# Delta rule: key and query products as half-array matmuls on the tiles where they lie, in place of keys copied into half-zero tiles

## The chip, the cores and the metric

One Trainium2 chip, one of its cores. A core has TensorE (PE in the rows, and PEld for its weight loads), VectorE (DVE), ScalarE (ACT), GpSimd (POOL) and SyncE (SP, which issues the transfers). The metric is the time of one execution on the device, in microseconds (us).

## The reference

Two blocks of two layers each, 512 positions wide. The change lies in the second block's mixer, in its third branch, the gated delta rule: 4 heads with keys, queries and values of 64 channels.

```
qc, kc, vc, bc, gc = (to_chunks(t) for t in (q, k, v, beta, g))
G = jnp.cumsum(gc, axis=-1)
L = jnp.exp(jnp.where(incl, G[..., :, None] - G[..., None, :], -jnp.inf))
kb = kc * bc[..., None]
A = jnp.where(strict, jnp.einsum('bnhtd,bnhsd->bnhts', kb, kc) * L, 0.0)
T = lax.linalg.triangular_solve(eye + A, eye, left_side=True, lower=True, unit_diagonal=True)
...
qk = jnp.where(incl, jnp.einsum('bnhtd,bnhsd->bnhts', qc, kc) * L, 0.0)
```

The two einsums, keys with keys and queries with keys, sum over the 64 channels of a head. They are what the change computes in another way. The kernel uses chunks of 128 positions, so there are 4 blocks (`b` from 0 to 3) of 4 heads (`h`).

## The kernel before

Each layer of the second block runs `second_mixer`: wide products with the weights, the second branch (`hgrn`), and then the third branch (`gdn`) woven with the first (`swa`, sliding window attention): `weave` takes one step of each generator in turn. Inside `gdn` the function `block(b)` runs for the four blocks, woven as well. The order of instructions on each engine is then set once, when the program is built, by a scheduler that works from its own estimates; on the chip each engine takes its list in that order.

Keys and queries lie with channels on the partitions: `k[0]` holds head 0 on partitions 0 to 63 and head 1 on 64 to 127, `k[1]` holds heads 2 and 3, and `q` likewise. The tiles in the rows are named `cout`. To keep the other head out of a sum over 128 partitions, the kernel copies each head's keys into a tile of its own, whose other 64 partitions are zero: `kz`, named `gk` in the rows, zeroed by GpSimd at L1400 and filled by ScalarE at L1401.

`block(b)` then does, step by step: transposes of the cumulated gates (L1438), the decay `e` (L1441 on VectorE, L1442 on ScalarE; `ge` in the rows), keys with keys (L1450), `am` from them (L1452; `gm` in the rows), transposes of `am` (L1457) with two selecting copies (L1458, L1459), queries with keys (L1463), their product with the decay (L1464), transposes of that (L1468, copied out by ScalarE at L1469), and then six doubling steps of the triangular inverse (L1476 with a copy L1477, L1481 with L1482, L1487 with L1488), all of them full 128x128 products.

Each step takes one tile from the PSUM pool `mm`, which has four tiles of 128x512 in turn: a step's products can't start before the tile that was taken four times earlier has been read out. `swa` has a pool of its own (`mx`, four tiles). Its lines in the rows: scores L1121, mask and maximum on VectorE (L1124, L1126), small vectors L1131 to L1134, the exponentials on ScalarE (L1138), normalising (L1140, L1141, L1143), transposes L1158 with copies L1160, and products with the values L1167, which use the 64 columns of one half of the array (128*64 in the rows).

A matmul of 128x128 in float32 stands as two rows' worth of records: the 16 products of L1450 in a layer are 32 records, and so are the 16 of L1463.

`hgrn`, which runs earlier in each layer, already has products of half the array: L1273 multiplies partitions 0 to 63 into one PSUM tile and 64 to 127 into another (64*128 in the rows).

Of the kernel before, what the change touches and what calls it, by code (L numbers as in the profile page):

```python
# [13 lines left out]
ALU = mybir.AluOpType  # L14
# [3 lines left out]
P = 128  # L18
SEQ = 512
# [230 lines left out]
class Net:  # L250
# [1095 lines left out]
    def gdn(self, x, cg, ba, l, out):  # L1346
        nc, V, G = self.nc, self.nc.vector, self.nc.gpsimd
        T = nc.tensor
# [14 lines left out]
        ps = self.ps("mm")  # L1363
# [24 lines left out]
        for i in range(2, 4):  # L1388
            ps = early.spread2(rn[:, :, 2 * i:2 * i + 2])
# [3 lines left out]
        rq = self.small((P, NB, 4), "grq", 2)  # L1393
        V.tensor_scalar(rq, rn[:, :, 0:4], 0.125, None, op0=ALU.mult)
        q, k, vf = x[0:2], x[2:4], x[4:6]
        kz2 = [self.big((P, 2, SEQ), "gk") for _ in range(2)]
        kz = [kz2[h // 2][:, h % 2, :] for h in range(4)]
        for h, t in enumerate(kz):
            r, n = slice(64 * (h % 2), 64 * (h % 2) + 64), slice(64 - 64 * (h % 2), 128 - 64 * (h % 2))
            G.memset(t[n, :], 0.0)  # L1400
            nc.scalar.copy(t[r, :], k[h // 2][r, :])  # L1401

        eb = self.small(sh, "geb", 2)
        V.tensor_tensor(eb, beta, eg, op=ALU.mult)
# [1 line left out]
        for i in range(2):  # L1406
            hh = slice(2 * i, 2 * i + 2)
            bc = lambda y: y[:, :, hh].unsqueeze(3).to_broadcast([P, NB, 2, 64])
            r = self.big((P, NB, 2, 128), name="grhs")
            ps = early.to_f([vf[i][:, b * P:(b + 1) * P] for b in range(NB)])  # L1410
            v4 = ps.rearrange("p (a b c) -> p a b c", a=NB, b=2)
            V.tensor_tensor(r[:, :, :, 0:64], v4, bc(beta), op=ALU.mult)
            ps = early.to_f([k[i][:, b * P:(b + 1) * P] for b in range(NB)])
            k4 = ps.rearrange("p (a b c) -> p a b c", a=NB, b=2)
            V.tensor_tensor(r[:, :, :, 64:128], k4, bc(eb), op=ALU.mult)
            t = self.t((P, NB, 2, 64), name="gkd")
# [9 lines left out]
        nb = self.small(sh, "gnb", 2)  # L1426
        V.tensor_scalar(nb, beta, -1.0, None, op0=ALU.mult)
        p4 = lambda y: y.rearrange("p (a b) -> p a b", a=4)
# [5 lines left out]
        def block(b):  # L1434
            s = slice(b * P, (b + 1) * P)
            ps = self.ps()
            for h in range(4):
                T.transpose(ps[:, h * P:(h + 1) * P], gc[:, b, h:h + 1].to_broadcast([P, P]), self.ident)  # L1438
            e = self.t((P, 4, P), name="ge")
            for h in range(4):  # L1440
                V.scalar_tensor_tensor(e[:, h, :], ps[:, h * P:(h + 1) * P], gc[:, b, h:h + 1], later, op0=ALU.subtract, op1=ALU.max)  # L1441
            nc.scalar.activation(out=e, in_=e, func=AF.Exp, scale=-1.0)  # L1442
            r0 = self.wp.tile([P, 2, 4, P], F32, tag="whi", name=self.nm("gm0"))
            r1 = self.wp.tile([P, 2, 4, P], F32, tag="wlo", name=self.nm("gm1"))
            xx, xt, am, zt = r0[:, 0], r0[:, 1], r1[:, 0], r1[:, 1]
            nc.sync.dma_start(out=r0.rearrange("p a b c -> p (a b) c"), in_=self.ident.unsqueeze(1).to_broadcast([P, 8, P]))
            yield
            ps = self.ps()
            for h in range(4):
                T.matmul(ps[:, h * P:(h + 1) * P], kz[h][:, s], kz[h][:, s], start=True, stop=True)  # L1450
            for h in range(4):
                V.scalar_tensor_tensor(am[:, h, :], ps[:, h * P:(h + 1) * P], nb[:, b, h:h + 1], e[:, h, :], op0=ALU.mult, op1=ALU.mult)  # L1452
            yield

            ps = self.ps()
            for h in range(4):
                T.transpose(ps[:, h * P:(h + 1) * P], am[:, h, :], self.ident)  # L1457
            V.copy_predicated(xx, all4(off1).bitcast(I32), am)  # L1458
            V.copy_predicated(xt, all4(lvs[0]).bitcast(I32), p4(ps))  # L1459
            yield  # L1460
            ps = self.ps()
            for h in range(4):
                T.matmul(ps[:, h * P:(h + 1) * P], q[h // 2][:, s], kz[h][:, s], start=True, stop=True)  # L1463
            V.tensor_tensor(e, p4(ps), e, op=ALU.mult)  # L1464
            yield
            ps = self.ps()
            for h in range(4):
                T.transpose(ps[:, h * P:(h + 1) * P], e[:, h, :], self.ident)  # L1468
            nc.scalar.copy(e, p4(ps))  # L1469
            QT[b] = e  # L1470
            yield

            for n in range(1, 7):
                ps = self.ps()
                for h in range(4):
                    T.matmul(ps[:, h * P:(h + 1) * P], am[:, h, :], xt[:, h, :], start=True, stop=True)  # L1476
                nc.scalar.copy(zt, p4(ps))  # L1477
                yield
                ps = self.ps()
                for h in range(4):  # L1480
                    T.matmul(ps[:, h * P:(h + 1) * P], xx[:, h, :], zt[:, h, :], start=True, stop=True)  # L1481
                V.copy_predicated(xt, all4(lvs[n]).bitcast(I32), p4(ps))  # L1482
                yield
                if n < 6:
                    ps = self.ps()
                    for h in range(4):
                        T.transpose(ps[:, h * P:(h + 1) * P], xt[:, h, :], self.ident)  # L1487
                    nc.scalar.copy(xx, p4(ps))  # L1488
                yield
            ps = self.ps()  # L1490
            for h in range(4):
                T.matmul(ps[:, h * P:(h + 1) * P], xt[:, h, :], rhs[h // 2][:, b, h % 2, :], start=True, stop=True)
            t = self.t((P, 4, P), name="guw", tag="x")
            nc.scalar.copy(t, p4(ps))
            uw[b] = t
            yield
            if b:
                ps = self.ps()
                for h in range(4):
                    p = h % 2  # L1500
                    T.matmul(ps[64 * p:64 * p + 64, (h // 2) * P:(h // 2 + 1) * P], rhs[h // 2][:, b, p, 64:128], xt[:, h, :], start=True, stop=True)
                for i in range(2):
                    nc.scalar.copy(wt[i][:, s], ps[:, i * P:(i + 1) * P])
            yield

        yield from weave(*(block(b) for b in range(NB)))

        sbd = {}
        for i in range(2):
            state = None  # L1510
            for c in range(NB - 1):
                ps = self.ps("mx")
                for p in range(2):
                    r = slice(64 * p, 64 * p + 64)
# [6 lines left out]
                else:  # L1521
                    m = self.t((P, P), name="gmt", tag="x")
                    G.memset(m, 0.0)
                    for p in range(2):
                        r = slice(64 * p, 64 * p + 64)
                        V.scalar_tensor_tensor(m[r, r], self.ident[r, r], gl[r, c, 2 * i + p:2 * i + p + 1], ps[r, 64 + 64 * p:128 + 64 * p],
                                               op0=ALU.mult, op1=ALU.subtract)
# [10 lines left out]
                for p in range(2):  # L1538
                    r = slice(64 * p, 64 * p + 64)
# [3 lines left out]
        for b in range(NB):  # L1543
            s = slice(b * P, (b + 1) * P)
# [15 lines left out]
            else:  # L1560
                t = self.t((P, 4, 64), name="got", tag="x")
                V.tensor_tensor(t, o3(po[:, 256:512]), eg[:, b, :].unsqueeze(2).to_broadcast([P, 4, 64]), op=ALU.mult)
                V.tensor_tensor(hs[:, 0], t, o3(p2[:, 0:256]), op=ALU.add)
            r = self.head_rstd(hs, (1, 4), rq[:, b:b + 1, :])
# [299 lines left out]
```

## Time and profile before

| | us |
|---|---|
| median of 3 runs | 3590.18 (3586.36 to 3591.63) |
| profiled execution, its time | 3586.55 |
| profiled execution, its span | 3584.7 |
| L1450 in one layer, TensorE | 5.51 |
| L1401 in one layer, ScalarE | 2.54 |
| L1400 in one layer, GpSimd | 2.24 |

The span runs from the first to the last instruction; 1.85 us of the profiled execution's time lie around it. The stage of the change comes twice, from 2296 us (first layer of the second block) and from 3035 us (its second layer). Rows name engine, line, operation, the tile written and those read, and in brackets the idle time of the engine before it and what ended it.

### The profile page before, as it was taken

How to read it: one execution, taken by the hardware profiler on the slowest of the kernel's cores; microseconds unless marked ns; L12 is line 12 of the kernel's file. 1: busy time of each engine (PE TensorE's matmuls, PEld its weight loads, DVE VectorE, ACT ScalarE, POOL GpSimd, SP SyncE). 2: the span in 40 equal slices, each digit the busy share in tenths (PEclk: the TensorE clock that was granted, in tenths of full speed). 3: DMA queues.
4: the chain of work that ended last, by engine and by line, in shares of the span. 5: the costliest groups of instructions: out<-in, count | busy, mean ns of one | idle time of the engine just before them, and what ended most of it. 6: DMA issues, size and time to landing. Idle time of an engine off the chain costs nothing.

```text
span 3584.7 us, 44503 instructions
## 1 busy us (share of the span) xinstructions
PE 3484.3 (97%) x17694; PEld 2901.8 (81%) x17694; DVE 1989.1 (55%) x3074; ACT 1364.5 (38%) x2231; POOL 140.5 (4%) x130
## 2 busy tenths in 40 slices
PE   9999999999999999999999998899999989999999
PEld 7888777888888888777888887788888877888887
DVE  6555665554665555674556577756333475654333
ACT  4223454323333223463223364354222453543221
POOL 0000000000000000000000003100000021000000
PEclk9999999999999999999999999899999999999999
DMA  5444212444334443202444321102333222022332
GB/s 167 141 135 129 84 32 68 142 145 128 127 100 142 146 138 100 91 15 95 146 148 137 94 77 54 62 7 75 108 98 101 78 71 68 1 71 90 100 99 83
DMA packets 114272, 349.06 MB, mean 97 GB/s; under 512 B 11536, under 2 KB 27920, under 8 KB 114064
## 3 DMA queue, kind: packets, MB, share of 16 engines
q1 hardware_dynamic: 114064, 346.21, 30.8%
q8 instruction: 140, 2.29, 0.3%
q14 instruction: 68, 0.56, 0.0%
HBM read 339.87 MB, written 2.10 MB: 95 GB/s over the span
## 4 chain that ended last, share of the span: by engine, by line
PE 87%; DVE 6%; issue 3%; ACT 2%; POOL 1%; DMA 1%; SPq 0%; POOLq 0%; DVEq 0%; ACTq 0%
PE mm L406 24%; PE mm L408 24%; PE mm L407 24%; PE mm L1481 1%; PE mm L1476 1%; PE mm L476 1%; PE mm L477 1%; PE mm L475 1%; PE mx L968 1%; DVE hacc L1279 1%; DVE wlo L382 1%; PE mm L809 1%; PE mx L948 1%; ACT sc L1138 1%; PE mx L1121 1%
## 5 line engine op out<-in xcount | busy, mean ns | idle before, releaser
L381 ACT CAST whi<-wraw 128x1024 fp32r<-128x1024 f32 (+3 forms) x540 | 553.4, 1029 | 1553.6 <-PE mm L407 1271.7
L406 PE MATMUL mm<-xh,whi 128*128 128x512 f32 (+1 forms) x2784 | 1053.3, 380 | 9.7 <-ACT whi L381 6.4
L407 PE MATMUL mm<-xl,whi 128*128 128x512 f32 (+1 forms) x2784 | 1055.8, 380 | 1.6 <-DVE xl L588 1.4
L408 PE MATMUL mm<-xh,wlo 128*128 128x512 f32 (+1 forms) x2784 | 1055.8, 380 | 0.3 <-DVE wlo L382 0.3
L382 DVE TENSOR_TENSOR wlo<-wraw,whi 128x1024 fp32r<-128x1024 f32 (+3 forms) x540 | 643.7, 1194 | 274.9 <-ACT whi L381 234.3
L406 PEld LDWEIGHTS mm<-xh,whi 128*128 128x128 f32 x2784 | 522.4, 189 | 107.8 <-ACT whi L381 6.4
L407 PEld LDWEIGHTS mm<-xl,whi 128*128 128x128 f32 x2784 | 524.9, 189 | 100.3 <-DVE xl L588 2.5
L408 PEld LDWEIGHTS mm<-xh,wlo 128*128 128x128 f32 x2784 | 524.8, 189 | 100.4 <-DVE wlo L382 3.1
L408 PE MATMUL mm<-hi,wlo 128*128 128x512 f32 (+1 forms) x1390 | 532.2, 383 | 2.1 <-DVE wlo L382 2.1
L406 PE MATMUL mm<-hi,whi 128*128 128x512 f32 (+1 forms) x1390 | 532.5, 384 | 0.2
L407 PE MATMUL mm<-lo,whi 128*128 128x512 f32 (+1 forms) x1390 | 531.8, 383 | 0.0
L408 PEld LDWEIGHTS mm<-hi,wlo 128*128 128x128 f32 x1390 | 261.3, 188 | 54.2 <-DVE wlo L382 4.2
L406 PEld LDWEIGHTS mm<-hi,whi 128*128 128x128 f32 x1390 | 261.1, 188 | 51.4 <-ACT hi L399 1.1
L407 PEld LDWEIGHTS mm<-lo,whi 128*128 128x128 f32 x1390 | 261.3, 188 | 50.3
L658 DVE SCALAR_TENSOR_TENSOR h<-mm,h 128x512 f32<-128x512 f32 x112 | 77.2, 691 | 224.2 <-PE mm L408 224.1
L1589 DVE SCALAR_TENSOR_TENSOR ada<-wraw,cond,ada 128x1024 f32<-128x1024 f32 x84 | 107.9, 1284 | 95.6 <-DMA wraw<-in_ada_w_dram 95.2
L637 DVE TENSOR_TENSOR gl<-mm,rstd 128x512 f32<-128x512 f32 x88 | 60.7, 690 | 155.1 <-PE mm L408 155.1
L636 DVE TENSOR_TENSOR silu<-mm,rstd 128x512 f32<-128x512 f32 x88 | 60.7, 689 | 145.2 <-PE mm L408 145.2
L658 DVE SCALAR_TENSOR_TENSOR h<-mm,mod,h 128x512 f32<-128x512 f32 (+1 forms) x70 | 48.9, 704 | 148.7 <-PE mm L408 148.7
L399 ACT CAST hi<-gl 128x512 fp32r<-128x512 f32 x132 | 82.2, 623 | 100.6 <-DVE gl L639 99.9
L633 DVE TENSOR_TENSOR gl<-silu,mm 128x512 f32<-128x512 f32 x44 | 30.2, 687 | 135.8 <-PE mm L408 135.8
L400 DVE TENSOR_TENSOR lo<-gl,hi 128x512 fp32r<-128x512 f32 x132 | 90.5, 686 | 15.4 <-ACT hi L399 15.4
(493 smaller groups left out, 3606.2 us busy)
## 6 DMA issues: line engine op xcount, KB each, us to landing
wraw<-in_ffn_gate_dram SPq DMA_DIRECT2D x130, 512.0 KB, 3.5
wraw<-in_ffn_up_dram SPq DMA_DIRECT2D x130, 512.0 KB, 4.0
wraw<-in_ada_w_dram SPq DMA_DIRECT2D x96, 512.0 KB, 3.7
wraw<-in_ffn_down_dram SPq DMA_DIRECT2D x96, 448.0 KB, 3.3
wraw<-in_win_f_dram SPq DMA_DIRECT2D x50, 512.0 KB, 3.5
wraw<-in_ffn_down_dram SPq DMA_DIRECT2D x48, 512.0 KB, 3.5
wraw<-in_w_out_dram SPq DMA_DIRECT2D x32, 512.0 KB, 3.5
wraw<-in_win_t_dram SPq DMA_DIRECT2D x16, 512.0 KB, 3.5
```

Of the source, the lines that this page charges most:

```text
L381: self.nc.scalar.copy(hi[:, s], raw)
L382: self.nc.vector.tensor_tensor(lo[:, s], raw, hi[:, s].bitcast(F32), op=ALU.subtract)
L399: self.nc.scalar.copy(hi, src)
L400: self.nc.vector.tensor_tensor(lo, src, hi.bitcast(F32), op=ALU.subtract)
L406: T.matmul(ps, whi, xhi, start=first, stop=False)
L407: T.matmul(ps, whi, xlo, start=False, stop=False)
L408: T.matmul(ps, wlo, xhi, start=False, stop=last)
L475: T.matmul(ps, xh[:, bs], w[0][:, s], start=k == 0, stop=False)
L636: nc.vector.tensor_tensor(sg, gate_ps, rb, op=ALU.mult)
L637: nc.vector.tensor_tensor(gg, up_ps, rb, op=ALU.mult)
L658: self.nc.vector.scalar_tensor_tensor(h, ps[:, c], scale, h, op0=ALU.mult, op1=ALU.add)
L1589: V.scalar_tensor_tensor(acc, raw, cond[:, k:k + 1], acc, op0=ALU.mult, op1=ALU.add)
```

## The change

The copies `kz` with their memsets go. Keys with keys and queries with keys are taken by a helper `scores`, which multiplies 64 partitions of `k[i]` or `q[i]` with the same 64 of `k[i]`. The two halves write into two PSUM tiles, so a step that took one tile of the pool now takes two, each half filled. Head `h` then lies in tile `h % 2` at column block `h // 2`; the four VectorE operations at L1452 read from there, and L1464 becomes two operations of 128x256 on every second head in place of one of 128x512. Behind the helper the lines are numbered by 4 and less more; the helper's matmul is L1403.

```
-        kz2 = [self.big((P, 2, SEQ), "gk") for _ in range(2)]
-        kz = [kz2[h // 2][:, h % 2, :] for h in range(4)]
-        for h, t in enumerate(kz):
-            r, n = slice(64 * (h % 2), 64 * (h % 2) + 64), slice(64 - 64 * (h % 2), 128 - 64 * (h % 2))
-            G.memset(t[n, :], 0.0)
-            nc.scalar.copy(t[r, :], k[h // 2][r, :])
+        half = slice(0, 64), slice(64, 128)
+        def scores(x, y, s):
+            pss = [self.ps() for _ in range(2)]
+            for i in range(2):
+                for r, ps in zip(half, pss):
+                    T.matmul(ps[:, i * P:(i + 1) * P], x[i][r, s], y[i][r, s], start=True, stop=True)
+            return [ps[:, 0:2 * P].rearrange("p (a b) -> p a b", a=2) for ps in pss]
...
-            ps = self.ps()
+            pss = scores(k, k, s)
             for h in range(4):
-                T.matmul(ps[:, h * P:(h + 1) * P], kz[h][:, s], kz[h][:, s], start=True, stop=True)
-            for h in range(4):
-                V.scalar_tensor_tensor(am[:, h, :], ps[:, h * P:(h + 1) * P], nb[:, b, h:h + 1], e[:, h, :], op0=ALU.mult, op1=ALU.mult)
+                V.scalar_tensor_tensor(am[:, h, :], pss[h % 2][:, h // 2, :], nb[:, b, h:h + 1], e[:, h, :], op0=ALU.mult, op1=ALU.mult)
...
-            ps = self.ps()
-            for h in range(4):
-                T.matmul(ps[:, h * P:(h + 1) * P], q[h // 2][:, s], kz[h][:, s], start=True, stop=True)
-            V.tensor_tensor(e, p4(ps), e, op=ALU.mult)
+            for ps, y in zip(scores(q, k, s), (e[:, 0:4:2, :], e[:, 1:4:2, :])):
+                V.tensor_tensor(y, ps, y, op=ALU.mult)
```

The first place is on TensorE, at the queries with keys of blocks 2 and 3. Before, `mm_17610` is block 2, `mm_17622` block 3, both whole; `ge` are the transposes of L1468, `sc` and `pt` belong to `swa`:

```order
L1463 MATMUL mm_17610<-gk_17275,cout_16971 128x128 x2
L1463 MATMUL mm_17610<-gk_17276,cout_17012 128x128 x2
L1463 MATMUL mm_17622<-gk_17275,cout_16971 128x128 x2
L1463 MATMUL mm_17622<-gk_17276,cout_17012 128x128
L1121 MATMUL mx_17616<-kz_17251,u_16788 128x256
L1121 MATMUL mx_17616<-kz_17254,u_16788 128x256
L1463 MATMUL mm_17622<-gk_17276,cout_17012 128x128
L1468 MATMUL mm_17650<-base,ge_17350 128x128 x4
L1158 MATMUL mx_17657<-base,sc_17399 128x128 x2
L1158 MATMUL mx_17668<-base,sc_17419 128x128 x4
L1167 MATMUL mx_17656<-pt_17660,av_15674 64x128
L1468 MATMUL mm_17662<-base,ge_17386 128x128 x4
```

In the change the same place reads as follows; `mm_17608` and `mm_17609` are the two halves of block 2, `mm_17622` and `mm_17623` those of block 3:

```order
L1121 MATMUL mx_17616<-kz_17254,u_16788 128x256
L1403 MATMUL mm_17608<-cout_17053,cout_16971 128x128
L1403 MATMUL mm_17608<-cout_17094,cout_17012 128x128
L1158 MATMUL mx_17659<-base,sc_17389 128x128 x2
L1403 MATMUL mm_17609<-cout_17053,cout_16971 128x128
L1403 MATMUL mm_17609<-cout_17094,cout_17012 128x128
L1158 MATMUL mx_17670<-base,sc_17409 128x128 x4
L1167 MATMUL mx_17658<-pt_17662,av_15674 64x128
L1403 MATMUL mm_17622<-cout_17053,cout_16971 128x128
L1403 MATMUL mm_17622<-cout_17094,cout_17012 128x128
L1167 MATMUL mx_17658<-pt_17662,av_15674 64x128
L1158 MATMUL mx_17685<-base,sc_17429 128x128 x3
```

Block 3's second half, `mm_17623`, follows after these and stands between products of L1158. Before, two blocks stood in one run; now four half blocks stand one by one among full-array products, and the transposes of L1468 have moved behind them.

The second place is on VectorE, where `am` is made from the keys' products. Before, the rows of the first two blocks read:

```order
L1143 TENSOR_TENSOR sc_17342<-sc_17342,wr_17361 128x512
L1452 SCALAR_TENSOR_TENSOR gm_3283_17357<-mm_17442,gnb_17335,ge_17350 128x128 x4
L1124 TENSOR_TENSOR sc_17454<-mx_17451,mats_16874 128x512
L1452 SCALAR_TENSOR_TENSOR gm_3290_17393<-mm_17457,gnb_17335,ge_17386 128x128
L1126 TENSOR_REDUCE wm_17395<-sc_17454 128x2
```

And in the change:

```order
L1143 TENSOR_TENSOR sc_17332<-sc_17332,wr_17351 128x512
L1454 SCALAR_TENSOR_TENSOR gm_3281_17347<-mm_17432,gnb_17325,ge_17340 128x128
L1454 SCALAR_TENSOR_TENSOR gm_3281_17347<-mm_17433,gnb_17325,ge_17340 128x128
L1454 SCALAR_TENSOR_TENSOR gm_3281_17347<-mm_17432,gnb_17325,ge_17340 128x128
L1454 SCALAR_TENSOR_TENSOR gm_3281_17347<-mm_17433,gnb_17325,ge_17340 128x128
L1124 TENSOR_TENSOR sc_17445<-mx_17442,mats_16874 128x512
```

Here VectorE's work stays in its place, still behind the normalising products L1143; only the tiles read have become two.

## Rows read from the trace of the kernel before

**Rows 1.** The page's chain that ended last, shares of the span by engine

```profile
PE 87%; DVE 6%; issue 3%; ACT 2%; POOL 1%; DMA 1%; SPq 0%; POOLq 0%; DVEq 0%; ACTq 0%
```

**Rows 2.** Busy time by stretches; PE, PEld, DVE, ACT, POOL, granted clock, DMA share, GB/s

```profile
2296.00:2345.00 49.00, 36.28 (x240) 30.43 (x241) 44.27 (x107) 22.58 (x59) 6.86 (x4) 0.83 0.00 1
2345.00:2400.00 55.00, 53.40 (x480) 50.11 (x476) 23.52 (x48) 35.09 (x83) 1.23 (x5) 1.00 0.01 1
```

**Rows 3.** Chain in order of time: start, length, piece; a row of the inverse

```profile
2377.71 3.57 PE mm L1476 x32
```

**Rows 4.** Timeline of ScalarE at the copies: start, length, work, idle before

```profile
2301.54 2.54 ACT L1401 COPY gk<-cout 64x512 f32<-64x512 f32 x4
2307.17 0.63 ACT L843 ACTIVATE cout<-cacc 128x512 f32<-128x512 f32 x1 [3.09 <-DVE cacc L841]
```

**Rows 5.** Timeline of GpSimd at the memsets

```profile
2184.07 2.24 POOL L1400 MEMSET gk<- 64x512 f32 x4
2186.57 1.04 POOL L1260 TENSOR_TENSOR he<-hl 128x512 f32<-128x512 f32 x1 [0.25 <-DVE hk L1265]
```

**Rows 6.** Timeline, first layer, keys with keys and VectorE around them

```profile
2317.57 5.51 PE L1450 MATMUL mm<-gk 128*128 128x128 f32 x32 [1.95 <-ACT sc L1138]
2320.96 0.17 DVE L1140 TENSOR_TENSOR wr<-wr,we 128x8 f32<-128x8 f32 x1 [0.69 <-ACT sc L1138]
2324.10 1.12 DVE L1452 SCALAR_TENSOR_TENSOR gm<-mm,gnb,ge 128x128 f32<-128x128 f32 x4
2333.38 0.17 DVE L1140 TENSOR_TENSOR wr<-wr,we 128x8 f32<-128x8 f32 x1 [0.41 <-ACT sc L1138]
```

**Rows 7.** Timeline of TensorE, first layer, queries with keys and after

```profile
2337.67 0.94 PE L1463 MATMUL mm<-gk,cout 128*128 128x128 f32 x6 [2.28 <-DVE gm L1459]
2338.44 1.03 PE L1121 MATMUL mx<-kz,u 128*128 128x256 f32 x4
2339.31 0.38 PE L1463 MATMUL mm<-gk,cout 128*128 128x128 f32 x2
2341.08 0.43 PE L1167 MATMUL mx<-pt,av 128*64 128x128 f32 x2 [0.26 <-ACT pt L1160]
2346.65 2.84 PE L1476 MATMUL mm<-gm,gm 128*128 128x128 f32 x24
```

**Rows 8.** Timeline of TensorE in `hgrn`, one half-array run between full ones

```profile
2167.10 0.34 PE L475 MATMUL mm<-whi,xh 128*128 128x392 f32 x1
2167.37 1.16 PE L1273 MATMUL mx<-hq,hk 64*128 64x128 f32 x16
2168.47 0.44 PE L476 MATMUL mm<-wlo,xh 128*128 128x392 f32 x1
2168.75 0.34 PE L477 MATMUL mm<-whi,xl 128*128 128x392 f32 x1
2168.93 0.34 PE L475 MATMUL mm<-whi,xh 128*128 128x392 f32 x1
```

**Rows 9.** Timeline of weight loads where 128 and 64 columns change

```profile
2325.32 0.42 PEld L1158 LDWEIGHTS mx<-base,sc 128*128 128x128 f32 x4 [0.17 <-issue]
2325.90 0.41 PEld L1167 LDWEIGHTS mx<-pt,av 128*64 128x64 f32 x4 [0.17 <-issue]
```

**Rows 10.** Timeline of VectorE, one operation of 256 and one of 512

```profile
2338.09 0.43 DVE L1124 TENSOR_TENSOR sc<-mx,mats 128x256 f32<-128x256 f32 x1
2338.42 0.69 DVE L1464 TENSOR_TENSOR ge<-mm,ge 128x512 f32<-128x512 f32 x1
```

**Rows 11.** 2 us stretches of both layers, columns as in rows 2

```profile
2336.00:2338.00 2.00, 0.33 (x3) 0.33 (x4) 2.00 (x4) 0.00 (x0) 0.00 (x0) 1.00 0.00 0
3076.00:3078.00 2.00, 2.00 (x10) 1.71 (x10) 2.00 (x6) 0.00 (x0) 0.00 (x0) 0.66 0.00 0
```

**Rows 12.** Timeline of TensorE, second layer, same place as rows 7

```profile
3075.51 0.94 PE L1463 MATMUL mm<-gk,cout 128*128 128x128 f32 x6 [2.27 <-DVE gm L1459]
3085.80 2.84 PE L1476 MATMUL mm<-gm,gm 128*128 128x128 f32 x24
```

## The prediction

> **What bounds the kernel now.** I read the chain first: 87% of it is TensorE [rows 1], so time is saved or lost where TensorE's list gets shorter or longer, unless another engine is waited for at that place. The stage of the change is partly such a place, so I read it by stretches [rows 2]. From 2296 to 2345 us TensorE is busy for 36.28 of 49 us and VectorE for 44.27: here VectorE is ahead of TensorE as the bound. From 2345 to 2400 TensorE is busy for 53.40 of 55 us, and its chain runs record on record: 32 records of the inverse take 3.57 us, 0.112 each [rows 3]. What is late on TensorE when that second part begins is late at the end.
>
> The border between the two lies at the queries with keys. TensorE waits 2.28 us for VectorE's L1459, starts at 2337.67, and from then on has next to no gap [rows 7]. So each part of the change is priced by the side of 2337.67 on which it falls. The second layer has the same list and the same border, at 3075.51 [rows 12].
>
> **The copies that go.** L1401 takes 2.54 us of ScalarE, but the next work of ScalarE then waits 3.09 us for VectorE [rows 4]: worth nothing. L1400 takes 2.24 us of GpSimd, and the next L1260 starts when VectorE has read its tile, after a gap of 0.25 [rows 5]: worth nothing either. If that cover failed, the two would be worth at most 2.54 + 2.24 us a layer.
>
> **Keys with keys, before the border.** L1450 takes 5.51 us [rows 6]. It looks like the natural place for a gain, but the work behind it on VectorE doesn't start when it is done: VectorE waits for ScalarE's exponentials at 2320.96, then normalises, and takes up L1452 at 2324.10, a microsecond after the products have ended. The order on VectorE has not moved there. I take nothing. Two PSUM tiles a block mean that blocks 2 and 3 can't start before blocks 0 and 1 are read out by VectorE, where before all four were issued in one run. Block 3's products then have the time in which VectorE does block 2, four operations in 1.12 us, and take up to 1.30 (eight records and a change of shape and back, priced below): 0.2 us late. VectorE has 0.41 us in hand, in which it waits for ScalarE at 2333.38 [rows 6], so I take nothing; with that slack gone it is 0.2 us a layer.
>
> **Queries with keys, at and after the border.** Here order and trace together give the loss. Before, block 3 starts at 2337.67 and six of its eight records are out before L1121 can start at 2338.44; only two records, at 2339.31, cost anything after that: 2 x 0.112 = 0.22 us [rows 7]. In the change blocks 2 and 3 both lie behind the border, since their PSUM tiles are those of blocks 0 and 1, which L1464 must read first; and they lie there as four runs of two matmuls, each between products of another shape.
>
> What such a run costs, `hgrn` shows [rows 8]. From the start of the full product at 2167.10 to that of the second full one after the half-array run, at 2168.75, 1.65 us pass. Two full products of 392 columns are in it, 0.18 each (2168.75 to 2168.93). That leaves 1.29 for 16 half-array records. One by one they would take 1.79, yet the row has all 16 within 1.16, so they run in pairs, one from each half, 8 x 0.112 = 0.89; the other 0.40 is the price of going into the half shape and back. A run of four records, all from one half, has no partner to start with: 4 x 0.112 + 0.40 = 0.85 us. Four runs: 3.4 us. Less the 0.22 that was there: +3.2 us.
>
> The Trainium skill ("TensorEngine Tiling (Array Packing)", Theoretical Speedup) gives products whose sum runs over 64 or fewer up to twice the speed. The pairs of `hgrn` agree, 16 records in 1.16 us [rows 8]. By that rule these four runs would cost half, 4 x 0.22 = 0.9 us, and the change would cost 0.7 us a layer here and not 3.2; by the order printed above each run has one half only, so I go by the row.
>
> The order also breaks up `swa`'s products of 64 columns: seven runs of L1167 before the inverse in place of four, which is four changes of shape more, beside those already in the 0.40. A change costs TensorE 0.17 us [rows 9]: 0.7 us. Part of them fall where TensorE would wait anyway, and the wait of 0.26 for ScalarE [rows 7] goes; between 0 and 0.7 I take half, 0.35, less 0.26: +0.1. L1464 becomes two operations of 256: 2 x 0.43 - 0.69 = 0.17 us a block, 0.7 a layer on VectorE [rows 10]. It lies beside TensorE's longer list and costs nothing; without that cover it is 0.7.
>
> So +3.3 us a layer, +6.6 for two, and no stretch of TensorE's later list has a gap to swallow it [rows 2, 3].
>
> **The clock.** In the first layer TensorE is busy for only 0.33 us of the two before 2338 and keeps the clock of 2.4 GHz; in the second, at the same place, part of the stretch from 3076 runs at the level of 1.2 GHz (mean 0.66) [rows 11]. What that costs is in the rows: from the border to the inverse the first layer takes 2346.65 - 2337.67 = 8.98 us, the second 3085.80 - 3075.51 = 10.29, so 1.3 us [rows 7, 12]. The change moves two blocks' products out of the stretch ahead of the border, so TensorE does less there in both layers. I expect the first layer to lose its clock as the second does: +1.3. The same could happen after 2322, where TensorE now waits between the blocks of L1403; that is another 1.3 a layer at most, and I leave it to the range.
>
> **Sum.** 6.6 + 1.3 = 7.9 us. The profiled execution's 3586.55 us lie 3.63 below the median of the runs shown; against the median the forecast is 3590.18 + 7.9 = 3598.
>
> **Rivals.** *Hidden both ways*: the four runs fall into gaps between VectorE's operations. L1464's eight operations and the L1124 and L1126 between them pace that stretch too. For it speaks that VectorE is the busier engine up to 2345; against it that TensorE has one gap of 0.26 us there and none after. Then the change costs at most the 0.2 us a layer of the first stretch: 3590 to 3591.
>
> *The other side, faster*: the stretch of L1450 is TensorE's after all. The chain that ended last does pass through its 5.51 us. If halves paired up there and in L1463 as in `hgrn`, 64 records a layer would fall from 0.112 to 0.056: 3.6 us a layer, 7.2 in all, 3583. It decides itself at VectorE's first L1452: if that starts well before 2324.1, this is the case. VectorE's wait for ScalarE at 2320.96 speaks against it, and so does the order, which sets two matmuls of one half behind each other. The Trainium skill's rule of the twofold speed, named above, would give this case if TensorE were the bound.
>
> *Deeper loss*: the clock stays at 1.2 GHz from the waits between the blocks of keys with keys through to the inverse. Then to the 7.9 come 1.3 a layer after 2322, and the shape changes are dearer at half clock, up to 0.40 for each of the eight runs: 7.9 + 2.6 + 3.2 = 13.7, 3604.
>
> **How the numbers follow.** No change means within 0.2%, 7.2 us of 3590.18, about what a measurement of this kernel can tell. The forecast gets 0.62; its own range is +4 to +12 us, and it falls on both sides of 7.2: 0.39 slower, 0.23 the same. Hidden 0.20, all the same. Faster 0.08: 0.05 faster, 0.03 the same, since 7.2 is on the border. Deeper 0.10, slower. That is 0.05 faster, 0.46 same, 0.49 slower. The range runs from 3589, just below the hidden case, to 3604, the deeper one, and leaves out the faster case and what is beyond the deeper one, some 0.15.
>
> **What would show it.** Right: VectorE's first `am` at its old place; four separate runs of L1403 behind the border, each some 0.85 us from the product before to the product after; the inverse's first L1476 later against the border by 3 to 5 us in the first layer; granted clock below 1 around 2336 to 2342. Wrong: runs of L1403 that add less than 0.6 each, or TensorE idle between them for VectorE; `am` earlier than before; a later wait (TensorE's for L1488) that shrinks by as much as the stage grew.

## The result and the profile after

The changed kernel takes 3615.91 us (median of four runs, 3614.14 to 3620.5) against 3590.45 for the kernel before on the same chip: ratio 1.0078, 95% interval 1.0066 to 1.0089. It is 25 us slower. The forecast was 3598 with a range from 3589 to 3604; sign and place were right, the size was not.

The profiled run of after has a span of 3612.1 us, 27.4 more than before. The place is again the border between VectorE's part and TensorE's part of the stage: the wait of 2.71 us that VectorE's L1461 ends. TensorE in the first layer, at the border, at the inverse's first product and at L1492, the first product behind the inverse; then the same three in the second layer (answers to [rows 7, 12]):

```profile
2339.45 0.71 PE L1403 MATMUL mm<-cout,cout 64*128 64x128 f32 x4 [0.58 <-DVE gm L1461]
2342.87 1.22 PE L1403 MATMUL mm<-cout,cout 64*128 64x128 f32 x4 [2.71 <-DVE gm L1461]
2344.02 2.07 PE L1121 MATMUL mx<-kz,u 128*128 128x256 f32 x4
2346.03 1.22 PE L1403 MATMUL mm<-cout,cout 64*128 64x128 f32 x4
2347.18 0.69 PE L1158 MATMUL mx<-base,sc 128*128 128x128 f32 x2
2347.79 1.22 PE L1403 MATMUL mm<-cout,cout 64*128 64x128 f32 x4
...
2360.60 0.94 PE L1476 MATMUL mm<-gm,gm 128*128 128x128 f32 x6
2427.01 3.74 PE L1492 MATMUL mm<-grhs,gm 128*128 128x128 f32 x32
...
3093.76 1.22 PE L1403 MATMUL mm<-cout,cout 64*128 64x128 f32 x4 [2.71 <-DVE gm L1461]
3111.49 0.94 PE L1476 MATMUL mm<-gm,gm 128*128 128x128 f32 x6
3177.90 3.74 PE L1492 MATMUL mm<-grhs,gm 128*128 128x128 f32 x32
```

Before, L1492 stands here:

```profile
2411.37 3.74 PE L1492 MATMUL mm<-grhs,gm 128*128 128x128 f32 x32
3150.51 3.74 PE L1492 MATMUL mm<-grhs,gm 128*128 128x128 f32 x32
```

From the border to L1492 before takes 2411.37 - 2337.67 = 73.70 us and 3150.51 - 3075.51 = 75.00 [rows 7, 12]; after takes 84.14 in both layers: +10.44 and +9.14. L1492 is the better mark than L1476 here, since the change also moves the transposes L1468 partly behind the first L1476.

The border itself comes later. VectorE of after, where it makes `am` (L1454; before, L1452 of [rows 6]):

```profile
2326.79 1.12 DVE L1454 SCALAR_TENSOR_TENSOR gm<-mm,gnb,ge 128x128 f32<-128x128 f32 x4
...
2331.67 0.35 DVE L1454 SCALAR_TENSOR_TENSOR gm<-mm,gnb,ge 128x128 f32<-128x128 f32 x1 [1.47 <-PE mm L1403]
...
2334.47 1.12 DVE L1454 SCALAR_TENSOR_TENSOR gm<-mm,gnb,ge 128x128 f32<-128x128 f32 x4 [1.45 <-PE mm L1403]
```

The first `am` still follows L1143 without a wait, but VectorE then waits twice for L1403, of block 2 and of block 3. From the first `am` to the border: 2342.87 - 2326.79 = 16.08 us, before 2337.67 - 2324.10 = 13.57 [rows 6, 7], so +2.51. That is the two waits less the 0.41 us that VectorE had in hand [rows 6]: 1.47 + 1.45 - 0.41. The first `am` of the second layer, after and then before:

```profile
3077.62 1.12 DVE L1454 SCALAR_TENSOR_TENSOR gm<-mm,gnb,ge 128x128 f32<-128x128 f32 x4
```

```profile
3062.03 1.12 DVE L1452 SCALAR_TENSOR_TENSOR gm<-mm,gnb,ge 128x128 f32<-128x128 f32 x4
```

There it is 3093.76 - 3077.62 = 16.14 against 3075.51 - 3062.03 = 13.48, so +2.66.

The first layer's loss is 2.51 + 10.44 = 12.95, the second's 2.66 + 9.14 = 11.80: the two stages hold 24.75 of the 27.4 us. The rest lies ahead of the first layer's first `am`, 2326.79 against 2324.10; e3 and e6 below, which keep the copies, have it at 2326.45 and 2328.65, and no cause is shown for it.

What TensorE does there is in the windows of after: from 2298 us to the border, within that 10 us of keys with keys, and 15 us from the border on (columns as in [rows 2]):

```profile
2298.00:2342.87 44.87, 30.79 (x177) 24.02 (x177) 37.13 (x95) 17.01 (x48) 6.55 (x3) 0.72 0.00 1
2320.90:2331.10 10.20, 9.23 (x42) 6.73 (x44) 8.62 (x27) 6.20 (x16) 0.00 (x0) 0.50 0.00 0
2342.87:2357.87 15.00, 15.00 (x52) 10.18 (x53) 8.35 (x21) 2.13 (x4) 0.00 (x0) 0.50 0.00 0
```

Behind the border TensorE has work in all 15.00 us, and the granted clock is 0.50, 1.2 GHz, in all of them: 52 records. Another 10 us at that level lie ahead of it, while keys with keys run. Before, 17 us from the border have a clock of 1.00 in the first layer and 0.90 in the second:

```profile
2337.67:2354.67 17.00, 16.74 (x135) 14.85 (x136) 12.79 (x28) 11.34 (x30) 0.52 (x2) 1.00 0.01 1
3075.51:3092.51 17.00, 17.00 (x125) 15.04 (x126) 11.49 (x24) 10.48 (x29) 0.32 (x1) 0.90 0.00 1
```

The copies that went left waits of the same size: ScalarE's L843 now waits 5.54 us where it waited 3.09 [rows 4], and GpSimd's L1260 waits 2.57 where it waited 0.25 [rows 5]. After, ScalarE and then GpSimd:

```profile
2309.87 0.63 ACT L843 ACTIVATE cout<-cacc 128x512 f32<-128x512 f32 x1 [5.54 <-DVE cacc L841]
...
2188.98 1.04 POOL L1260 TENSOR_TENSOR he<-hl 128x512 f32<-128x512 f32 x1 [2.57 <-DVE hk L1265]
```

### The profile page after: what moved, and what is told of

Read it like the earlier page. It is cut to its first block, busy times and chain, and to the rows that moved or that the text cites. A ratio compares the mean times of both kernels' runs of the same rounds, so it can differ in the third digit from the quotient of the medians.

```text
span 3612.1 us, 44485 instructions
## 1 busy us (share of the span) xinstructions
PE 3508.6 (97%) x17694; PEld 2912.4 (81%) x17694; DVE 1990.0 (55%) x3082; ACT 1360.4 (38%) x2223; POOL 135.3 (4%) x122
## 4 chain that ended last, share of the span: by engine, by line
PE 87%; DVE 6%; issue 3%; ACT 2%; POOL 1%; DMA 1%; SPq 0%; POOLq 0%; DVEq 0%; ACTq 0%
PE mm L406 24%; PE mm L408 24%; PE mm L407 24%; PE mm L1481 1%; PE mm L1476 1%; PE mm L477 1%; PE mm L476 1%; PE mm L475 1%; PE mx L968 1%; DVE hacc L1279 1%; DVE wlo L382 1%; PE mm L809 1%; PE mx L1121 1%; PE mx L948 1%; PE mx L1158 1%
```

## Experiments

The change does three things to TensorE: a step takes two PSUM tiles (which also reorders its list), products have the half shape, and the granted clock falls. The theory is that the clock is the larger part of the loss; the rivals are tiles and order, and the price of changing the shape. "kk" is keys with keys, "qk" queries with keys. Each ratio is to the kernel before, measured beside the run.

| run | median us | ratio, 95% interval |
|---|---|---|
| e1 all full, two tiles a step | 3597.3 | 1.0025 (1.0016 to 1.0034) |
| e2 kk halves, qk as before | 3593.5 | 1.0008 (0.9999 to 1.0017) |
| e3 qk halves, kk as before | 3611.0 | 1.0061 (1.0047 to 1.0074) |
| e4 changed kernel, filler after every run | 3604.8 | 1.0043 (1.0029 to 1.0057) |
| e5 heads 0 and 2 halves, one tile | 3604.2 | 1.0044 (1.0030 to 1.0058) |
| e6 qk full, two tiles; kk as before | 3595.2 | 1.0018 (1.0009 to 1.0027) |
| e7 second half in swa's pool | 3602.9 | 1.0038 (1.0025 to 1.0050) |
| e8 before, copies twice | 3593.0 | 1.0012 (1.0004 to 1.0021) |
| e9 heads 0 and 2 over 65 partitions | 3591.8 | 1.0004 (0.9994 to 1.0013) |
| e10 halves, two blocks a pair of tiles | 3598.4 | 1.0024 (1.0015 to 1.0034) |
| e11 as e6, qk of blocks 2, 3 halves | 3606.5 | 1.0055 (1.0039 to 1.0071) |
| e12 as e6, qk of blocks 0, 1 halves | 3598.8 | 1.0029 (1.0020 to 1.0038) |
| e13 as e3, the wait filled | 3597.7 | 1.0018 (1.0008 to 1.0027) |
| e14 as e6, the wait filled | 3593.3 | 1.0011 (1.0002 to 1.0019) |
| e15 changed kernel, the wait filled | 3598.5 | 1.0025 (1.0015 to 1.0035) |
| e16 before, the wait filled | 3586.8 | 0.9988 (0.9979 to 0.9997) |

**Tiles and order without the half shape (e1).** The copies are kept and both operands are full again:

```
...
-                for r, ps in zip(half, pss):
-                    T.matmul(ps[:, i * P:(i + 1) * P], x[i][r, s], y[i][r, s], start=True, stop=True)
+                for p, ps in enumerate(pss):
+                    T.matmul(ps[:, i * P:(i + 1) * P], (x[i] if x is q else kz[2 * i + p])[:, s], kz[2 * i + p][:, s], start=True, stop=True)
```

> The copies of the keys stay, and every product is a full-array product again, but each step of scores writes two half-filled PSUM tiles: TensorE's list has the same order as in the changed kernel, row for row. Theory A (shape and clock): what costs 25 us is the half-array shape, by the changes into and out of it and by the stretches of 10.24 and 17.07 us at 1.2 GHz that come with it; with full products this kernel falls back to within 5 us of before, 3590 to 3595, and its trace shows 3.4 us at 1.2 GHz after 2318 and none of 17 us at the border. Theory B (tiles and order): what costs is that a step takes two of the four PSUM tiles, so that four runs lie behind the border, swa's products are broken up and TensorE waits between blocks; then it stays at 3610 to 3618, with the long stretches at 1.2 GHz in it.

3597.3: between the two, so tiles and order are a part, about 9 us, and shape with clock the larger one. VectorE of e1, first layer, where it waits for block 3's kk:

```profile
2331.74 1.13 DVE L1460 SCALAR_TENSOR_TENSOR gm<-mm,gnb,ge 128x128 f32<-128x128 f32 x4 [1.87 <-PE mm L1409]
```

TensorE of e1 at the border and at L1492 (here L1498):

```profile
2340.15 1.22 PE L1409 MATMUL mm<-gk,cout 128*128 128x128 f32 x4 [2.71 <-DVE gm L1467]
2418.10 3.74 PE L1498 MATMUL mm<-grhs,gm 128*128 128x128 f32 x32
```

The wait is there with full products too, so it comes from the list: block 3's products stand behind `swa`'s L1167 and L1121. From the border to L1498 it is 77.95, +4.25. That is not tiles and order alone: the clock is low for a while behind the border here too, and e14 below takes that out.

**One einsum at a time (e2, e3).** Each takes the other's lines from the kernel before, with its copies.

> Keys with keys alone as half-array products, queries with keys as before. From the border on TensorE's list is that of before. Theory A: the 10.24 us at 1.2 GHz from 2320.9 come with these products and lie beside VectorE's work, so little of it is seen: 3590 to 3596; if the clock that is lost here is what is still low behind the border, 3598 or more. Theory B: two tiles a step delay only blocks 2 and 3 by 0.2 us: 3590 to 3592.

> Queries with keys alone as half-array products, keys with keys as before. From the border on TensorE's list is that of the changed kernel. Theory A with the clock lost at the border itself: 17 us at 1.2 GHz in each layer, and most of the loss, 3606 to 3614. Theory A with the clock lost by keys with keys: the four runs at 2.4 GHz, +7 us, 3597. Theory B: as in the first kernel of this call, whatever that gives.

kk alone cost at most 6 us, by the interval perhaps nothing; qk alone cost 22. Together about as much as the change, so they add up. The later border is kk's. VectorE and TensorE of e2:

```profile
2328.55 1.12 DVE L1460 SCALAR_TENSOR_TENSOR gm<-mm,gnb,ge 128x128 f32<-128x128 f32 x4
```

```profile
2344.71 0.94 PE L1471 MATMUL mm<-gk,cout 128*128 128x128 f32 x6 [2.28 <-DVE gm L1467]
```

From the first `am` to the border e2 takes 16.16 us, +2.59 against before; e3 takes 2339.92 - 2326.45 = 13.47, as before. The list of e3 from the border on is that of the changed kernel.

**Shape and clock with the list held (e6, e11, e12).** e6 is to e3 as e1 to the changed kernel; e11 and e12 turn blocks into halves by one condition:

```
+                    if s.start >= 2 * P:   # e12: s.start < 2 * P
+                        T.matmul(ps[:, i * P:(i + 1) * P], x[i][half[p], s], y[i][half[p], s], start=True, stop=True)
+                    else:
...
```

> Queries with keys into two PSUM tiles a step but as full-array products; keys with keys as before. TensorE's list is that of the run with only queries with keys as halves, which took 3611.0. The difference of the two is the half shape and its clock alone. Theory A (clock): 3595 to 3598, order and tiles being 7 to 9 us of the 22. If tiles and order of queries with keys cost nothing and the loss of the first run of this study lay with keys with keys: 3589 to 3591. If the clock doesn't matter: 3608 or more.

> Queries with keys in two PSUM tiles a step, and of them only blocks 2 and 3, the four runs behind the border, as half-array products; blocks 0 and 1 and all keys with keys full. TensorE's list is that of the run with all queries with keys full in two tiles (3595.2) and of the run with all of them as halves (3611.0). If the half shape costs only its changes, 4 x 0.40 us a layer are added: 3598 to 3599. If the runs behind the border are also what keeps TensorE at 1.2 GHz there, most of the 15.8 us between those two runs comes: 3605 to 3611, with 10 us or more at 1.2 GHz behind the border.

> The counterpart: only blocks 0 and 1 of queries with keys as half-array products, of which all but one run of four records lie ahead of the border, where TensorE waits for VectorE; blocks 2 and 3 and all keys with keys full. Same list. If the loss comes from the runs behind the border: 3594 to 3599, near the run with all of them full, with 3.4 to 7 us at 1.2 GHz at the border. If the clock is already lost by the runs ahead of the border and then stays low whatever follows: 3603 to 3611.

One list, four versions: 3595.2 with no half, 3598.8 with blocks 0 and 1, 3606.5 with blocks 2 and 3, 3611.0 with all. The larger part of the loss sits in the runs behind the border. In e11 the run at the border itself is a full one and in e12 a half one, so it belongs to blocks 0 and 1: a fifth run, block 1's second half, that stands there beside the four of blocks 2 and 3. Windows of some 15 us from the border on, first of e6:

```profile
2342.13:2357.13 15.00, 14.98 (x104) 12.16 (x105) 8.06 (x21) 7.33 (x21) 0.32 (x1) 0.89 0.00 1
```

The same of e11:

```profile
2340.10:2355.00 14.90, 14.90 (x53) 10.31 (x54) 8.25 (x21) 2.13 (x4) 0.00 (x0) 0.50 0.00 0
```

The same of e12:

```profile
2339.80:2354.70 14.90, 14.90 (x96) 11.95 (x97) 8.15 (x21) 6.49 (x19) 0.32 (x1) 0.84 0.00 1
```

All three have lost the clock in the wait of 2.7 us ahead of the border. With full runs it soon comes back (0.89 over the window), and 104 records are done; with four half-array runs of four records it stays at 1.2 GHz throughout, and 53 are done in as much time, with TensorE just as busy.

**Filling the wait (e13, e14, e15).** If the half runs only keep the clock down, they do no harm where it has not fallen. Ten products that nobody reads go into the wait, behind block 1's first half; the same lines stand in all three:

```
+            if x is q and s.start == P:
+                for j in range(10):
+                    T.matmul(pss[0][:, (2 + j % 2) * P:(3 + j % 2) * P], x[j % 2][:, s], y[j % 2][:, s], start=True, stop=True)
```

> The run with only queries with keys as half-array products (3611.0), with ten full-array products of 128 columns put into TensorE's wait of 2.7 us ahead of the border, behind the first half of block 1, into columns that nobody reads: 20 records, 2.2 us a layer at 2.4 GHz. Behind the border the list is the same, four half-array runs. If those runs only keep the clock from coming back once the wait has taken it away, then without the fall they run at 2.4 GHz, 4 x 0.84 us, and the time is 3597 to 3602, with under 4 us at 1.2 GHz after the border. If the half-array runs themselves take the clock down, it falls behind the border all the same, and the time stays at 3608 to 3613.

> The same ten products in the same wait, with queries with keys as full-array products in two tiles (3595.2 without them): the same list on TensorE as its partner in this call. What it gains is the 3.4 to 6.8 us at 1.2 GHz that those runs show at the border, up to 1.7 us a layer: 3592 to 3595. The partner's distance from it is the price of the half shape without the clock: 2 x 4 x 0.40 = 3.2 us if the clock holds in both, 12 to 16 if it does not.

> The changed kernel itself, with the same ten full-array products of 128 columns in TensorE's wait ahead of the border, into columns that nobody reads; the rest of its list as it was. From the run of the same filler with queries with keys alone as halves: the clock then holds at the border, and what stays of the change is its later border, 2.5 us a layer, and the shape and order behind it, 3.6 us a layer: 12 us less the 1.3 that the kernel before loses of its own clock in the second layer, 3599 to 3603. If keys with keys as halves bring the fall to another place behind the border: 3606 to 3616.

With twenty records more to do in each layer e13 is 13 us faster than e3, and the changed kernel itself (e15) falls from 3615.9 to 3598.5, just below what was expected. TensorE in e15, the filler (L1406), the border, a half run and L1492 (here L1495):

```profile
2337.31 0.71 PE L1403 MATMUL mm<-cout,cout 64*128 64x128 f32 x4 [0.58 <-DVE gm L1464]
2337.95 2.50 PE L1406 MATMUL mm<-cout,cout 128*128 128x128 f32 x20
2340.74 0.71 PE L1403 MATMUL mm<-cout,cout 64*128 64x128 f32 x4 [0.29 <-DVE gm L1464]
2341.38 1.13 PE L1121 MATMUL mx<-kz,u 128*128 128x256 f32 x4
2342.44 0.71 PE L1403 MATMUL mm<-cout,cout 64*128 64x128 f32 x4
2343.08 0.44 PE L1158 MATMUL mx<-base,sc 128*128 128x128 f32 x2
...
2418.01 3.74 PE L1495 MATMUL mm<-grhs,gm 128*128 128x128 f32 x32
```

Windows of e15 from its border:

```profile
2340.74:2357.74 17.00, 17.00 (x119) 13.35 (x120) 9.54 (x25) 9.88 (x28) 0.32 (x1) 1.00 0.00 1
```

The clock is 1.00 over the same half runs, and a run takes 0.64 us to the next start, 2343.08 - 2342.44, where it took 1.15 in after, 2347.18 - 2346.03. Border to L1495: 77.27 us, +3.57 against before and 6.87 less than after. In e14, with full runs:

```profile
2341.32 0.71 PE L1409 MATMUL mm<-gk,cout 128*128 128x128 f32 x4 [0.48 <-DVE gm L1472]
2417.72 3.74 PE L1503 MATMUL mm<-grhs,gm 128*128 128x128 f32 x32
```

Here the way is 76.40 us, +2.70. So at 2.4 GHz tiles and order cost 2.70 a layer behind the border, and the half shape 3.57 - 2.70 = 0.87.

**More full work beside the halves (e4).** Two full products behind each half run, here with another list on TensorE:

```
+            for ps in pss:
+                for i in range(2):
+                    T.matmul(ps[:, 2 * P + i * P:3 * P + i * P], x[i][:, s], y[i][:, s], start=True, stop=True)
```

> The changed kernel with two more full-array products of 128 columns behind every half-array run, into the columns of the same PSUM tile that nobody reads: 32 more products, 64 records, 7.2 us of TensorE a layer at 2.4 GHz, and as many changes of shape. It computes nothing more that is used. If the clock follows how much of the array TensorE drives, the stretches at 1.2 GHz shrink: 3606 to 3618, about the changed kernel's time in spite of 14 us more work. If the loss is changes of shape or waits for tiles, the work comes on top: 3626 to 3640.

11 us faster than the changed kernel with 64 records more a layer, a shade below the expected range. It points the same way, but it also moves `swa`'s products and fills the wait, so alone it does not say which.

**The price of the shape (e5, e9).** With one tile and the list of before, the products of heads 0 and 2 are halves in e5; in e9 they read 65 partitions of the copies, one of them zero:

```
...
+        kz = [k[0][0:64], kz2[:, 0, :], k[1][0:64], kz2[:, 1, :]]   # e5
...
+        rows = slice(0, 65), slice(0, 128)                          # e9
+                T.matmul(ps[:, h * P:(h + 1) * P], kz[h][rows[h % 2], s], kz[h][rows[h % 2], s], start=True, stop=True)
...
```

> The kernel before, with one PSUM tile a step, in which the products of heads 0 and 2 are taken as half-array products on the keys where they lie and those of heads 1 and 3 stay full-array products on the half-zero copies. TensorE's list is that of before, row for row; every second product has the half shape, so there are 32 excursions into it a layer. If the half shape itself costs the 0.40 us an excursion that the prediction took from hgrn: up to 32 x 0.40 = 12.8 us a layer less what VectorE's work covers, 3600 to 3612. If the half shape is free at 2.4 GHz and what costs is order and clock (the four runs of a layer at 2.4 GHz took 0.64 us each from start to next start with the filler behind them): 3588 to 3593, and no stretch of 10 us or more at 1.2 GHz after 2318.

> The kernel before, in which the products of heads 0 and 2 read 65 partitions of the half-zero copies in place of 128: the 64 of the head and one of zeros. TensorE's list is that of before and of the mixed run. It tells apart what the mixed run (3604.2) paid for. If the change between the 64-partition shape and the full one is what costs, and 65 partitions still count as the full shape, the records read 128*128, two take 0.22 us at 2.4 GHz, and the time is that of before, 3587 to 3592. If it is the clock, and the clock follows how many partitions a product sums over, the long stretches at 1.2 GHz after 2318 stay without any change of shape: 3594 to 3604. If 65 partitions also make a change of shape: 3604.

e5 costs 15.6 us, e9 nothing that the interval tells. TensorE in e5's qk, full and half in turn (`gk` is a copy, the other rows read the keys where they lie):

```profile
2337.38 0.49 PE L1463 MATMUL mm<-gk,cout 128*128 128x128 f32 x2
2337.80 0.49 PE L1463 MATMUL mm<-cout,cout 64*128 64x128 f32 x2
2338.22 0.49 PE L1463 MATMUL mm<-gk,cout 128*128 128x128 f32 x2
```

Windows of e5's kk and of its qk:

```profile
2316.60:2330.10 13.50, 13.50 (x47) 9.57 (x48) 11.46 (x39) 5.43 (x15) 0.00 (x0) 0.50 0.00 0
2337.38:2341.97 4.59, 4.59 (x23) 3.25 (x22) 3.39 (x8) 1.17 (x5) 0.00 (x0) 1.00 0.00 0
```

Two records take 0.42 us where 0.22 were due: each change of shape costs 0.20 at 2.4 GHz, in and out 0.40, the price read from `hgrn`. The same alternation held 1.2 GHz for 13.50 us in kk, where it began after a wait, and 2.4 GHz in qk. So the reading in e5's expectation that the shape is free at 2.4 GHz is wrong for runs between full products, and no clock is needed to explain a good part of e5's loss. In e9 the first row of kk reads

```profile
2320.05 5.44 PE L1451 MATMUL mm<-gk 65*128 65x128 f32 x32 [2.26 <-ACT sc L1138]
```

32 records take 5.44 us, about as before (5.51) [rows 6]: 65 partitions show no price for a change of shape. The clock is at 1.00 again while e5's is at 0.50:

```profile
2324.10:2340.00 15.90, 13.10 (x106) 10.94 (x105) 15.56 (x42) 8.14 (x24) 0.00 (x0) 1.00 0.00 1
```

The short dip in the products of kk ahead of this window is one that the kernel before has too (0.50 from 2319.20 to 2322.20).

**Other ways to place the halves (e7, e10).** e7 takes the second tile from `swa`'s pool; e10 lets two blocks share the two tiles:

```
-            pss = [self.ps() for _ in range(2)]
+            pss = [self.ps(), self.ps("mx")]   # e7
...
+            if b % 2 == 0:                     # e10
+                both[what] = [self.ps() for _ in range(2)]
...
```

> The changed kernel with the second half of each step in a PSUM tile of swa's pool, so that a step takes one tile of either pool. TensorE's list changes: swa's scores come later, and queries with keys stand between L1468's transposes. If the pressure on the pool mm is what puts four runs behind the border and lets TensorE wait, this gains much of the loss back: 3595 to 3605. If it is the clock that the half shape loses, whatever the order, 3606 to 3618, with 10 us and more at 1.2 GHz in the stage.

> All products as half-array products on the tiles where they lie, as in the changed kernel, but two blocks share two PSUM tiles: one tile holds heads 0 and 2 of both blocks, the other heads 1 and 3. A block costs one tile again, and on TensorE's list all 16 keys-with-keys products are one run and all 16 queries-with-keys products one run, with one excursion into the half shape each and both halves side by side. If what the change lost is changes of shape, tiles and the clock that they cost: 32 records in pairs are 16 x 0.112 + 0.40 = 2.2 us in place of 3.6, the border isn't later than before, and the time is 3584 to 3592. If half-array products lose the clock however they are grouped, 10 us and more at 1.2 GHz after 2318 stay: 3596 to 3610.

e7 gains 13 us on the changed kernel, in the range given for the pressure on the pool. Its runs of qk no longer stand behind one long wait, and the clock is 0.99 from 2336 to 2353, though still 0.50 from 2322.6 to 2336.2; list and clock change together here, so it does not part the two. e10, with one run for each einsum, keeps 8 us of loss, in its second range: the wait ahead of the border is still 2.26 us, the run behind it has the half shape, and the clock is 0.50 from 2342.7 to 2352.9. The halves were not side by side all the way either: sixteen records took 1.71 us, where `hgrn`'s sixteen take 1.16 [rows 8],

```profile
2338.82 1.71 PE L1407 MATMUL mm<-cout,cout 64*128 64x128 f32 x16
```

since the list puts eight of one half behind eight of the other.

**The copies (e8), and before with the wait filled (e16).**

```
-        for h, t in enumerate(kz):
+        for h, t in enumerate(kz + kz):        # e8
...
+            if b == 2:                         # e16
+                for j in range(8):
+                    T.matmul(ps[:, 0:P], q[j % 2][:, s], k[j % 2][:, s], start=True, stop=True)
```

> The kernel before with its eight memsets and copies of keys done twice a layer: 2.5 us more of ScalarE and 2.2 us more of GpSimd a layer, nothing else. If the copies are hidden, as predicted: 3587 to 3590, the time of before. If either is on the path, up to 9.5 us more in all, 3598, and the change did gain as much by taking them away.

> The kernel before with eight such products ahead of block 2's queries with keys, where TensorE waits for VectorE, overwritten by the true ones. It can gain no more than what the second layer loses of its clock at the border, 1.3 us: 3588 to 3590, not to be told from before. If the products push block 2 behind L1464: a microsecond a layer more.

Twice the copies cost 4.4 us (1.4 to 7.5), which was not expected. GpSimd's second memsets now stand ahead of an L1260 without a gap:

```profile
2190.61 2.25 POOL L1400 MEMSET gk<- 64x512 f32 x4
2192.83 1.03 POOL L1260 TENSOR_TENSOR he<-hl 128x512 f32<-128x512 f32 x1
```

The one set was covered, with 0.25 us to spare [rows 5]; a second is not. ScalarE is still covered: in both layers L843 waits 0.47 us for VectorE behind the eight copies. That leaves GpSimd, and how its delay reaches the end was not traced. e16 is 0.12% faster than before (0.03 to 0.21%), by an interval that just leaves out no change. Its window from the second layer's border has a clock of 1.00 where before had 0.90, and from there to L1492 (here L1495) it takes 73.70 us in both layers where before took 75.00 in the second, worth the 1.3 us; the rest of its 3.3 us lies within the interval and was not traced to a place.

## Why the prediction was wrong, step by step

- *The copies: worth nothing.* Right, as far as the waits show. The time taken away came back as waits, 3.09 to 5.54 us on ScalarE and 0.25 to 2.57 on GpSimd.
- *Keys with keys: nothing, 0.2 us a layer at most.* Wrong: the border is 2.51 and 2.66 us late. The step that failed is "Block 3's products then have the time in which VectorE does block 2". They do not start when their tiles come free; on TensorE's list they stand behind `swa`'s runs, and TensorE works through these at 1.2 GHz. e1 shows the wait for block 3 at full shape (1.87 us in both layers); its wait for block 2 is nothing in the first layer and 0.44 in the second, and with the halves (e2) 1.50 and 1.54.
- *Behind the border: +3.3 us a layer.* The sum came out, its parts did not, and that is luck. With the clock held (e15) it is 3.57: 2.70 for tiles and order, where the prediction's parts leave 1.7, and 0.87 for the half shape, where it had 1.6 for the changes of shape of the four runs. It left out block 1's second half, the run at the border, and counted seven runs of L1167 before the inverse where the trace has six ahead of the first L1476. Next to L1167, which has a shape of its own, a change has to be paid anyway: in e14 a full run ahead of it takes the same 0.64 us.
- *The clock: +1.3 us, first layer only.* This is the term that failed: 6.9 us a layer, in both. I priced a fall by the one that the kernel before has among full products, where the clock soon returns. Here half runs lie right behind the fall, and the clock does not return until they are done: the last starts at 2353.20, and the granted clock is 0.50 up to 2358 and 0.89 in the two us after. At 1.2 GHz a run takes 1.15 us to the next start in place of 0.64, and the stretch is over 15 us of dense TensorE work.
- *Rivals.* What happened is the "deeper loss", with a chance of 0.10: the clock is low at keys with keys and from the border to the inverse, with some 10 us at 2.4 GHz between. It was priced at 13.7 us by the same wrong step, stretches of 1.3 us, in place of the length of the stretch. Hidden and faster are out: TensorE is behind in both layers, and e10, with grouped halves, is 8 us slower than before. Halves do pair in the changed kernel where both tiles are free at once, against the prediction's reading of the order: eight records of block 3's keys with keys take 0.71 us at 2333.65, as long as a run of four at 2339.45. VectorE waits 1.45 us for block 3 all the same.

The account: 2.51 + 2.66 for the later border, 2 x 3.57 for shape and order, 2 x 6.87 for the clock behind the border, less the 1.3 that before loses in its second layer: 24.75 us, against 25.5 by the medians.

What stays open is why the half runs keep the clock down. e9 against e5, the same alternation with 65 partitions in place of 64, speaks against the number of partitions read. That it is the pauses at the changes of shape was not shown by itself, and e10, where one half run stands behind the fall and the clock is still 0.50 up to 2352.9, does not fit their number alone.

## What to carry to other kernels

Work that takes less of the array was not cheaper here in short runs among full products, and the half-zero copies, which other waits hid, cost nothing that the rows show. Before breaking TensorE's list into other shapes, look at what stands just ahead: here a wait of 2.71 us followed by such runs left the clock at 1.2 GHz for the dense stretch behind. Price a fall by the records that lie under it, not by the last fall that was seen. Where a wait can't be removed, try a few useless full products in it: here twenty records a layer were worth 17 us (e15).

## What the runs showed of the hardware

- A TensorE that the trace shows as busy did not get 2.4 GHz back: 15.00 us busy of 15.00 at 0.50 in after, and the same list behind the border with full runs at 0.89 (e6). The Trainium skill ("TensorE: Matmul & The Clock Gate", What's actually happening) has the throttle as the default and activity as what releases it. Here being busy by the trace was not enough for 15 us, and the shapes of the products made the difference; the measurement decides.
- Where the clock was up, it stayed up over the same half runs (1.00 over 17 us in e15). So one list ran at either level, by what stood ahead of it.
- A change between the 64-partition and the full shape cost 0.20 us at 2.4 GHz. The Trainium skill ("TensorEngine Tiling (Array Packing)", Key Properties) says that a switch of mode drains TensorE. The price in e5 agrees with that, though no run shows the drain itself. Products over 65 partitions paid none (e9).
